# Weight sums and rotary products of the second layer moved from GpSimd to VectorE

## The chip, the cores and the metric

The kernel runs on one core of a Trainium2 chip. The core has five engines with instruction queues of their own, each executed in order: TensorE (matrix products, PE in the profile, its weight loads PEld), VectorE (DVE), ScalarE (ACT), GpSimd (POOL) and SyncE (SP, which issues the DMAs here). The metric is the device time of one execution in microseconds; the medians are over several runs.

## What is computed

One inference step of a two-layer encoder over 2048 prompt tokens and 32 sample tokens, model width 1024. Layer one is a gated delta rule; then one shared K and V are projected from the stream; layer two is sliding-window attention with its own query and gate projections. The part that matters here is the projection in front of layer two:

```python
kv = h @ w_kv                                   # 1024 -> 512 (K 256, V 256)
k = rope_partial(kv[..., :256].reshape(b, l, 4, 64), pos)
...
proj = x @ w_in                                 # 1024 -> 2048
q = rope_partial(proj[..., :1024].reshape(b, l, 16, 64), pos) * (64 ** -0.5)
z = proj[..., 1024:]                            # gate, used as silu(z)
...
rot = jnp.concatenate([x1 * cos - x2 * sin, x2 * cos + x1 * sin], -1)   # rope_partial, 16 of 64 dims
```

## The kernel before

Prompt and sample tokens are one matrix of 2080 rows, cut into five blocks of 416 columns once transposed. The projection multiplies 20 weight tiles (1024 x 128 each: two for K, two for V, eight for the queries, eight for the gate) with these blocks. Every fp32 product is made of three matmuls on rounded halves, high by high, high by low and low by high (`multiply`, L1685 to L1687); the high half is a rounding cast and the low half is the difference to it. For weights the cast is on ScalarE (`cast`, L1370, w_hi) and the difference on VectorE (`rest`, L1358, w_lo); for activations likewise (`operand`, L1443 and again L1358: tiles b11h, t4l and so on).

Four of the five blocks are done in two pairs by a seven-product scheme of the Strassen kind. Two weight tiles and a pair of blocks form one *group* (`group`): seven products P1 to P7 in place of eight, over sums of weights and sums of activations. The weight sums of a group are `sum6` (two additions into the tiles s1 and s2, both named s in the trace, L1492 and L1493), `sum7` (L1497, in place in w_raw) and `sum3` (L1501, in place in w_raw). The activation sums are made ahead (`presum`, L1401, GpSimd) and kept in memory as s_sums. There are 10 groups for each pair, 20 in all, and the fifth block is done by plain products in between (`single`).

The products accumulate in three PSUM banks, X, Y and Z. When one is ready, ScalarE copies it (`copied`, L1513) or VectorE adds it to an earlier copy (`added`, L1518), and `finish` sends the tile on: K and query tiles with rotated rows through `regroup` and `rope`, V tiles through a transpose (`turn`, L1747), gate tiles through a tanh and L1709. `rope` shuffles the rows (L1735, VectorE), multiplies the shuffled rows with the sine table (L1736, GpSimd) and the rows with the cosine table (L1737, VectorE), asks for the next table (L1727; its tile cs has one buffer) and adds both (L1741, VectorE).

The order is written out by hand: inside `manual_schedule` each engine executes its instructions in the order in which the program emits them. `stream` walks through the list of products. At product p it emits the weight fetch for products up to 12 ahead, the sums of product p + 5, the cast of p + 3 and the low half of p + 2, then the matmuls, then what follows a product (`after`), then two steps of side work (operands of the coming pair, activation sums), then what `delay` has made due. So a sum is emitted two products ahead of the cast that reads it, whichever engine makes it. Beside all this, 16 tiles of the output weights are split, with a difference on GpSimd (`out_weights`, L1675, shown under L1358 as wo_parts).

The first pair's operands are built while its first products run (about 1305 to 1350 us of the trace), the second pair's from about 1475 to 1518 us, and the last group ends near 1690 us; attention follows.

Of the kernel before, what the change touches and what calls it, by code (L numbers as in the profile page):

```python
# [15 lines left out]
ALU = mybir.AluOpType  # L16
# [1282 lines left out]
class P2:  # L1299
# [7 lines left out]
    K, V, Q, Z = 0, 2, 4, 12  # L1307
# [169 lines left out]
    def group(self, i, pair):  # L1477


        c, d = self.PAIRS[pair]  # L1480
        nc, V, P, f = self.nc, self.nc.vector, self.nc.gpsimd, self.scale(i)
        u = types.SimpleNamespace(tiles=(i, i + 1), raws=[], o={}, s={})
        a, b = slice(0, 4), slice(4, 8)

        def raw(n, ks):
            return lambda: u.raws[n][:, ks]

        def sum6():
            r1, r2 = u.raws
            for t in ("s1", "s2"):  # L1490
                u.s[t] = self.wsums.tile([128, 4, 128], F32, tag=t, name=t)
            P.tensor_tensor(out=u.s["s1"][:], in0=r2[:, a], in1=r2[:, b], op=ALU.add)  # L1492
            P.tensor_tensor(out=u.s["s2"][:], in0=u.s["s1"][:], in1=r1[:, a], op=ALU.subtract)  # L1493

        def sum7():
            r1, r2 = u.raws
            P.tensor_tensor(out=r2[:, a], in0=r1[:, a], in1=r2[:, a], op=ALU.subtract)  # L1497

        def sum3():
            r1, r2 = u.raws  # L1500
            P.tensor_tensor(out=r1[:, b], in0=r1[:, b], in1=u.s["s2"][:], op=ALU.subtract)  # L1501

        def bank(name):
            def get():
                if name not in u.o:
                    pool = {"X": self.px, "Y": self.py, "Z": self.pz}[name]
                    u.o[name] = pool.tile([128, 512], F32, tag=name, name=name)
                return u.o[name][:, :TB]
            return get

        def copied(key):
            t = u.o[key] = self.out()
            nc.scalar.activation(t[:], u.o["X"][:, :TB], AF.Copy, scale=f)  # L1513
            return t

        def added(name, key, j, b):
            t = u.o.pop(key)
            V.scalar_tensor_tensor(out=t[:], in0=u.o[name][:, :TB], scalar=f, in1=t[:], op0=ALU.mult, op1=ALU.add)  # L1518
            self.finish(t, j, b)

        def after7():
            copied("u3")
            self.delay(lambda: added("Z", "u3", i + 1, d), 1)

        def new(act, n, src, name, start, after=None, sum=None):
            return self.product(u, n, src, lambda: self.x[act], bank(name), start, True, after, sum, (pair, act))

        return {
            "P1": new("b11", (0,), raw(0, a), "X", True, lambda: copied("p1")),
            "P2": new("b21", (0,), raw(0, b), "Y", True, lambda: added("Y", "p1", i, c)),  # L1530
            "P6": new("t2", (0, 1), lambda: u.s["s2"][:], "X", False, lambda: copied("u2"), sum6),
            "P5": new("t1", (), lambda: u.s["s1"][:], "Z", True),
            "P7": new("t3", (0, 1), raw(1, a), "X", False, after7, sum7),
            "P4": new("t4", (1,), raw(1, b), "X", False, lambda: self.finish(copied("c"), i + 1, c)),
            "P3": new("b22", (0,), raw(0, b), "Z", False, lambda: added("Z", "u2", i, d), sum3)}

    def groups(self, pair):
# [191 lines left out]
    def rope(self, a, n):  # L1729
        nc, V, cs = self.nc, self.nc.vector, self.cs  # L1730
        s = self.out()
        mask = [(i + 8) % 16 + i // 16 * 16 for i in range(32)]

        def products():
            V.stream_shuffle(s[:n], a[:n], mask)  # L1735
            nc.gpsimd.tensor_tensor(out=s[:n], in0=s[:n], in1=cs[:n, 1, :], op=ALU.mult)  # L1736
            V.tensor_tensor(out=a[:n], in0=a[:n], in1=cs[:n, 0, :], op=ALU.mult)  # L1737
            self.load_tables()

        self.delay(products, 1)  # L1740
        self.delay(lambda: V.tensor_tensor(out=a[:n], in0=a[:n], in1=s[:n], op=ALU.add), 2)  # L1741
        return 3
# [839 lines left out]
```

## Time and profile before

| | us |
|---|---|
| median of 3 runs | 2078.54 |
| lowest and highest | 2074.08, 2079.13 |
| the profiled execution | 2077.04 |
| its span, first to last instruction | 2075.2 |
| granted TensorE clock, mean | 0.992 |

The profile gives each engine's busy time and share of the span. A row of the timeline has the start, the time taken, engine, line, operation, out<-in, the shape and, in brackets, how long the engine had been idle and which instruction released it; rows of like instructions that follow each other are merged, with the time from the first start to the last end. A row of the waits has the total, the number and the longest. A row of a tile has the minimum, median and maximum of one instruction in ns and the first and last start in us. PEclk is the clock that TensorE was granted, 1.00 being full speed.

### The profile page before, as it was taken

How to read it: one execution, taken by the hardware profiler on the slowest of the kernel's cores; microseconds unless marked ns; L12 is line 12 of the kernel's file. 1: busy time of each engine (PE TensorE's matmuls, PEld its weight loads, DVE VectorE, ACT ScalarE, POOL GpSimd, SP SyncE). 2: the span in 40 equal slices, each digit the busy share in tenths (PEclk: the TensorE clock that was granted, in tenths of full speed). 3: DMA queues.
4: the chain of work that ended last, by engine and by line, in shares of the span. 5: the costliest groups of instructions: out<-in, count | busy, mean ns of one | idle time of the engine just before them, and what ended most of it. 6: DMA issues, size and time to landing. Idle time of an engine off the chain costs nothing.

```text
span 2075.2 us, 36940 instructions
## 1 busy us (share of the span) xinstructions
PE 2023.8 (98%) x13518; PEld 1853.7 (89%) x13518; DVE 1483.4 (71%) x2580; ACT 994.0 (48%) x2445; POOL 907.5 (44%) x1248
## 2 busy tenths in 40 slices
PE   8999999999999999999899998899989999999998
PEld 6999999999999999999888887899989997777775
DVE  4686667675646778888887897887878755666565
ACT  4444443446532267777673222534634445555552
POOL 0222222222223167777760123387255524566665
PEclk9999999999999999999999999999999999999999
DMA  5122333237666545545864999788767679433321
GB/s 210 53 82 79 113 97 113 88 99 225 200 172 186 181 144 173 172 161 174 287 234 127 261 248 256 265 248 292 266 213 240 201 213 312 116 104 107 103 73 66
DMA packets 355541, 360.82 MB, mean 174 GB/s; under 512 B 157584, under 2 KB 280240, under 8 KB 355344
## 3 DMA queue, kind: packets, MB, share of 16 engines
q1 hardware_dynamic: 348880, 344.03, 54.1%
q10 hardware_dynamic: 6480, 14.44, 1.9%
q8 instruction: 106, 1.74, 0.3%
q14 instruction: 75, 0.61, 0.1%
HBM read 235.54 MB, written 134.06 MB: 178 GB/s over the span
## 4 chain that ended last, share of the span: by engine, by line
PE 75%; DVE 8%; DMA 7%; issue 3%; POOL 2%; SPq 2%; ACT 2%; DVEq 0%; POOLq 0%; ACTq 0%
PE ps L79 12%; PE ps L81 12%; PE ps L80 12%; PE ot L1136 3%; PE ot L1137 3%; PE ot L1138 3%; PE S L2029 2%; PE ot L2062 2%; PE tr L2044 2%; PE X L1687 2%; PE X L1685 2%; PE X L1686 2%; DMA r<-in_x 2%; PE g L698 2%; DMA act_raw<-s_sums 1%
## 5 line engine op out<-in xcount | busy, mean ns | idle before, releaser
L79 PE MATMUL ps<-act_hi,w_hi 128*128 128x416 f32 x1280 | 455.1, 356 | 0.0
L81 PE MATMUL ps<-act_hi,w_lo 128*128 128x416 f32 x1280 | 449.8, 352 | 0.0
L80 PE MATMUL ps<-act_lo,w_hi 128*128 128x416 f32 x1280 | 448.0, 350 | 0.0
L79 PEld LDWEIGHTS ps<-act_hi,w_hi 128*128 128x128 f32 x1280 | 240.3, 188 | 4.2 <-issue 0.6
L80 PEld LDWEIGHTS ps<-act_lo,w_hi 128*128 128x128 f32 x1280 | 240.7, 188 | 3.1
L81 PEld LDWEIGHTS ps<-act_hi,w_lo 128*128 128x128 f32 x1280 | 240.1, 188 | 3.3
L212 DVE SCALAR_TENSOR_TENSOR y<-R,convw,y 128x2083 f32<-128x2083 f32 x72 | 185.1, 2572 | 62.6 <-ACT y L209 46.7
L56 POOL TENSOR_TENSOR w_lo<-w_raw,w_hi 128x1024 fp32r<-128x1024 f32 x25 | 62.6, 2503 | 320.7 <-ACT w_hi L55 295.4
L732 POOL TENSOR_TENSOR tm<-L,Tt 128x60 f32<-128x60 f32 (+19 forms) x365 | 132.4, 363 | 83.9 <-issue 40.6
L1863 POOL TENSOR_TENSOR P<-e,sm 128x384 f32<-128x384 f32 (+2 forms) x128 | 102.5, 822 | 118.9 <-DVE sm L1853 112.7
L734 POOL TENSOR_TENSOR Tt<-Tt,tm 128x60 f32<-128x60 f32 (+19 forms) x365 | 141.3, 387 | 28.6
L1849 ACT ACTIVATE e<-S,nm 128x193 f32<-128x193 f32 (+2 forms) x260 | 104.8, 416 | 96.7 <-DVE nm L1844 58.1
L1358 DVE TENSOR_TENSOR w_lo<-w_raw,w_hi 128x512 fp32r<-128x512 f32 x132 | 141.6, 1089 | 8.8 <-POOL w_hi L1370 5.1
L308 ACT COPY R<-ps 128x416 f32<-128x416 f32 (+1 forms) x144 | 60.3, 442 | 105.7 <-PE ps L81 93.8
L1513 ACT ACTIVATE o<-X 128x416 f32<-128x416 f32 x80 | 41.5, 518 | 133.5 <-PE X L1687 133.4
L1136 PE MATMUL ot<-wo,g_hi 128*128 128x512 f32 x256 | 103.7, 405 | 0.0
L1137 PE MATMUL ot<-wo,g_hi 128*128 128x512 f32 x256 | 100.8, 394 | 0.0
L1138 PE MATMUL ot<-wo,g_lo 128*128 128x512 f32 x256 | 100.7, 394 | 0.0
L1370 ACT CAST w_hi<-w_raw 128x512 fp32r<-128x512 f32 x129 | 76.6, 615 | 17.3 <-POOL w_raw L1501 8.9
L218 DVE SCALAR_TENSOR_TENSOR y<-th,y 128x2083 f32<-128x2083 f32 x24 | 55.9, 2328 | 37.6 <-ACT th L216 37.6
L1844 DVE TENSOR_REDUCE nm<-S 128x4 f32<-128x772 f32 (+3 forms) x66 | 60.6, 918 | 15.3 <-PE S L2029 15.3
L216 ACT ACTIVATE th<-y 128x2083 f32<-128x2083 f32 x24 | 46.7, 1948 | 50.8 <-DVE y L212 47.6
(369 smaller groups left out, 5218.3 us busy)
## 6 DMA issues: line engine op xcount, KB each, us to landing
w_raw<-in_b_w SPq DMA_DIRECT2D x60, 512.0 KB
w_raw<-in_w_in SPq DMA_DIRECT2D x40, 512.0 KB
act_raw<-s_hT SPq DMA_DIRECT2D x64, 208.0 KB
s_rows<-o SPq DMA_DIRECT2D x50, 208.0 KB
k<-s_k SPq DMA_DIRECT2D x17, 512.0 KB
E<-s_E SPq DMA_DIRECT2D x17, 512.0 KB
s_hT<-hT SPq DMA_DIRECT2D x65, 128.0 KB
s_bq<-s_rows SPq DMA_DIRECT2D x40, 208.0 KB
```

Of the source, the lines that this page charges most:

```text
L79: nc.tensor.matmul(ps, hi[:, k, :], xh[:, k, :], start=(k == 0), stop=False)
L80: nc.tensor.matmul(ps, hi[:, k, :], xl[:, k, :], start=False, stop=False)
L81: nc.tensor.matmul(ps, lo[:, k, :], xh[:, k, :], start=False, stop=(k == KC - 1))
L212: nc.vector.scalar_tensor_tensor(out=y[:], in0=R[:, j:j + W], scalar=self.convw[:, i, j:j + 1], in1=y[:], op0=ALU.mult, op1=ALU.add)
L732: P.tensor_tensor(out=tm[:n, i0 - k:, :w], in0=L[:n, i0:, j:j + 1].to_broadcast(sh), in1=Tt[:n, j:j + 1, :w].to_broadcast(sh), op=ALU.mult)
L734: P.tensor_tensor(out=Tt[:n, i0:, :w], in0=Tt[:n, i0:, :w], in1=tm[:n, i0 - k:, :w], op=ALU.subtract)
L1136: nc.tensor.matmul(ps[:n], ghi[:, k, :n], hi, start=a, stop=False)
L1137: nc.tensor.matmul(ps[:n], ghi[:, k, :n], lo, start=False, stop=False)
L1138: nc.tensor.matmul(ps[:n], glo[:, k, :n], hi, start=False, stop=z)
L1358: P.tensor_tensor(out=lo, in0=raw, in1=hi, op=ALU.subtract)
L1849: self.nc.scalar.activation(x.e[:, h, u, :x.n], x.S[:, h, u, :], AF.Exp, bias=x.nm[:, h, u:u + 1], scale=1.0, accum_out=x.sm[:, h, u:u + 1])
L1863: self.nc.gpsimd.tensor_tensor(out=x.P[:, u, :nj * 128].rearrange("r (j h k) -> r j h k", h=2, k=64), in0=x.e[:, :, u, :n].rearrange("r h ...
```

## The change

The four weight sums of a group and the product with the sine table are issued on VectorE instead of GpSimd. Shapes, operands, buffers and the place in the program stay.

```diff
-        nc, V, P, f = self.nc, self.nc.vector, self.nc.gpsimd, self.scale(i)
+        nc, V, f = self.nc, self.nc.vector, self.scale(i)
...
-            P.tensor_tensor(out=u.s["s1"][:], in0=r2[:, a], in1=r2[:, b], op=ALU.add)
-            P.tensor_tensor(out=u.s["s2"][:], in0=u.s["s1"][:], in1=r1[:, a], op=ALU.subtract)
+            V.tensor_tensor(out=u.s["s1"][:], in0=r2[:, a], in1=r2[:, b], op=ALU.add)
+            V.tensor_tensor(out=u.s["s2"][:], in0=u.s["s1"][:], in1=r1[:, a], op=ALU.subtract)
...
-            P.tensor_tensor(out=r2[:, a], in0=r1[:, a], in1=r2[:, a], op=ALU.subtract)
+            V.tensor_tensor(out=r2[:, a], in0=r1[:, a], in1=r2[:, a], op=ALU.subtract)
...
-            P.tensor_tensor(out=r1[:, b], in0=r1[:, b], in1=u.s["s2"][:], op=ALU.subtract)
+            V.tensor_tensor(out=r1[:, b], in0=r1[:, b], in1=u.s["s2"][:], op=ALU.subtract)
...
             V.stream_shuffle(s[:n], a[:n], mask)
-            nc.gpsimd.tensor_tensor(out=s[:n], in0=s[:n], in1=cs[:n, 1, :], op=ALU.mult)
+            V.tensor_tensor(out=s[:n], in0=s[:n], in1=cs[:n, 1, :], op=ALU.mult)
             V.tensor_tensor(out=a[:n], in0=a[:n], in1=cs[:n, 0, :], op=ALU.mult)
```

VectorE's queue in the first pair, where the last operands (t4l) are made and the second group's first sums fall due (about 1335 us of the trace before; s_14079 and s_14080 are that group's s1 and s2):

```order
 L1735 STREAM_SHUFFLE o<-o 64x416
+L1736 TENSOR_TENSOR o<-o,cs 64x416
 L1737 TENSOR_TENSOR o<-o,cs 64x416
 L1358 TENSOR_TENSOR w_lo<-w_raw,w_hi 128x512
 L1358 TENSOR_TENSOR t4l<-act_raw,t4h 128x416 x2
 L1741 TENSOR_TENSOR o<-o 64x416
+L1492 TENSOR_TENSOR s_14079<-w_raw 128x512
+L1493 TENSOR_TENSOR s_14080<-s_14079,w_raw 128x512
 L1358 TENSOR_TENSOR w_lo<-w_raw,w_hi 128x512
```

The product stands between the shuffle and L1737, and the two sums stand ahead of the next low half.

VectorE's queue of the changed kernel at the end of the second pair's operands (about 1507 us of the trace before), ahead of which stands the last L1709:

```order
L1735 STREAM_SHUFFLE o<-o 64x416
L1736 TENSOR_TENSOR o<-o,cs 64x416
L1737 TENSOR_TENSOR o<-o,cs 64x416
L1358 TENSOR_TENSOR w_lo<-w_raw,w_hi 128x512
L1358 TENSOR_TENSOR t4l<-act_raw,t4h 128x416 x2
L1741 TENSOR_TENSOR o<-o 64x416
L1358 TENSOR_TENSOR w_lo<-w_raw,w_hi 128x512
L1358 TENSOR_TENSOR t4l<-act_raw,t4h 128x416
```

Against before, only L1736 is new in these rows; the next two sums come behind the four b22l that follow.

GpSimd's queue in the first pair (about 1414 to 1430 us), with the s1 and s2 of one group as s_14931 and s_14932:

```order
 L1401 TENSOR_TENSOR act_raw<-act_raw 128x416 x2
 L1358 TENSOR_TENSOR wo_parts<-wo_parts 128x512
-L1736 TENSOR_TENSOR o<-o,cs 128x416
-L1501 TENSOR_TENSOR w_raw<-w_raw,s_14768 128x512
-L1492 TENSOR_TENSOR s_14931<-w_raw 128x512
-L1493 TENSOR_TENSOR s_14932<-s_14931,w_raw 128x512
-L1497 TENSOR_TENSOR w_raw<-w_raw 128x512
 L1401 TENSOR_TENSOR act_raw<-act_raw 128x416 x2
 L1358 TENSOR_TENSOR wo_parts<-wo_parts 128x512
```

Activation sums and output weights follow each other directly, and nothing else is left in that stretch. The queues of TensorE, ScalarE and SyncE are the same before and after.

## The prediction

> **What bounds the kernel now.** I read the page first, then the busy time by stretch, then what TensorE waits for, then both engines of the change in order of time.
>
> ```profile
> span 2075.2 us, 36940 instructions
> PE 2023.8 (98%) x13518; PEld 1853.7 (89%) x13518; DVE 1483.4 (71%) x2580; ACT 994.0 (48%) x2445; POOL 907.5 (44%) x1248
> ```
>
> TensorE sets the time. The change can only win what TensorE loses in the stage that holds the edited lines. Busy time by stretch (PE, PEld, DVE, ACT, POOL, granted clock, DMA share, GB/s):
>
> ```profile
> 1335.00:1352.00 17.00, 12.41 (x56) 11.38 (x55) 13.84 (x18) 7.78 (x16) 7.49 (x4) 0.90 0.90 316
> 1415.00:1447.00 32.00, 30.93 (x158) 28.93 (x157) 24.86 (x24) 14.03 (x28) 22.75 (x16) 1.00 0.84 293
> 1475.00:1505.00 30.00, 29.38 (x154) 28.17 (x153) 23.82 (x42) 21.29 (x45) 3.77 (x3) 1.00 0.85 281
> 1505.00:1520.00 15.00, 9.56 (x41) 8.62 (x40) 13.74 (x21) 7.54 (x15) 4.84 (x3) 0.89 0.72 225
> 1535.00:1543.00 8.00, 5.79 (x29) 5.06 (x29) 5.09 (x7) 2.18 (x4) 5.95 (x3) 1.00 0.36 111
> 1543.00:1690.00 147.00, 147.00 (x780) 145.62 (x779) 109.64 (x132) 64.06 (x126) 75.62 (x50) 1.00 0.67 210
> ```
>
> The last row gives TensorE's undisturbed pace: 147.00 / 780 = 0.1885 us a matmul. A stretch loses its length less its matmuls times 0.1885: 17 - 56 x 0.1885 = 6.4; 2.2; 1.0; 7.3; 2.5. Together **19.4 us, the ceiling**. From 1543 on nothing is lost, so there a later GpSimd or VectorE costs and wins nothing. Who holds TensorE up between 1300 and 1700:
>
> ```profile
> PE X L1687 <- DVE w_lo L1358: 5.5, 4, 2.5
> PE ps L1687 <- DVE w_lo L1358: 5.4, 2, 2.8
> PE Z L1685 <- DVE o L1518: 2.7, 2, 2.1
> ```
>
> VectorE, late with the low halves of the weights and with emptying bank Z. Why it is late shows in the instructions on the weights (minimum/median/maximum ns), in GpSimd's product, and in a VectorE line that reads one operand from PSUM:
>
> ```profile
> L1358 DVE TENSOR_TENSOR w_lo<-w_raw,w_hi x132: 640/686/1808, 1304.6 to 1727.3; 128x512 fp32r<-128x512 f32 x132
> L1492 POOL TENSOR_TENSOR s<-w_raw x20: 1279/1642/1754, 1315.5 to 1658.8; 128x512 f32<-128x512 f32 x20
> L1501 POOL TENSOR_TENSOR w_raw<-w_raw,s x20: 1289/1677/1753, 1325.8 to 1670.2; 128x512 f32<-128x512 f32 x20
> L1736 POOL TENSOR_TENSOR o<-o,cs x15: 1485/1503/2097, 1335.4 to 1612.9; 128x416 f32<-128x416 f32 x10, 64x416 f32<-64x416 f32 x5
> L1518 DVE SCALAR_TENSOR_TENSOR o<-Z,o x40: 575/591/593, 1345.4 to 1688.8; 128x416 f32<-128x416 f32 x40
> ```
>
> The same subtraction takes 0.64 or 1.81 us, while L1518 never stretches: a VectorE operation with two SBUF inputs stands still while GpSimd runs one. The place at 1335, on VectorE, GpSimd, ScalarE and TensorE:
>
> ```profile
> 1334.60 0.62 DVE L1735 STREAM_SHUFFLE o<-o 64x416 f32<-64x416 f32 x1
> 1335.26 0.58 DVE L1737 TENSOR_TENSOR o<-o,cs 64x416 f32<-64x416 f32 x1
> 1335.77 0.68 DVE L1358 TENSOR_TENSOR w_lo<-w_raw,w_hi 128x512 fp32r<-128x512 f32 x1
> 1336.37 4.30 DVE L1358 TENSOR_TENSOR t4l<-act_raw,t4h 128x416 fp32r<-128x416 f32 x2
> 1340.60 0.57 DVE L1741 TENSOR_TENSOR o<-o 64x416 f32<-64x416 f32 x1
> 1341.10 0.67 DVE L1358 TENSOR_TENSOR w_lo<-w_raw,w_hi 128x512 fp32r<-128x512 f32 x1
> 1345.40 0.58 DVE L1518 SCALAR_TENSOR_TENSOR o<-Z,o 128x416 f32<-128x416 f32 x1
> ```
> ```profile
> 1335.36 2.04 POOL L1736 TENSOR_TENSOR o<-o,cs 64x416 f32<-64x416 f32 x1 [8.23 <-DMA act_raw<-s_hT]
> 1338.73 1.50 POOL L1493 TENSOR_TENSOR s<-s,w_raw 128x512 f32<-128x512 f32 x1
> ```
> ```profile
> 1341.19 0.61 ACT L1370 CAST w_hi<-w_raw 128x512 fp32r<-128x512 f32 x1
> ```
> ```profile
> 1341.82 0.46 PE L1687 MATMUL X<-t4h,w_lo 128*128 128x416 f32 x1 [2.53 <-DVE w_lo L1358]
> 1346.13 0.43 PE L1685 MATMUL Z<-b22h,w_hi 128*128 128x416 f32 x1 [2.06 <-DVE o L1518]
> ```
>
> Two t4l subtractions need 4.30 us (1.0 without company) because GpSimd operations run one after another through them (the first and the third are shown).
>
> **The change, part by part.** Twenty groups have four sums each, and there are 15 products: 95 instructions leave GpSimd. None issues a DMA; the order of ScalarE, SP and TensorE stays.
>
> *Price on VectorE.* No sum on VectorE is in this trace; the same shape, two SBUF inputs, is w_lo, whose successor starts 0.60 us after it (1335.77, 1336.37). A 416-wide operation costs 0.50 to 0.51 (1340.60, 1341.10). Where the second reads what the first wrote, it waits for the end, as L1741 would: 0.69 for the sum pair. So 80 x 0.62 + 15 x 0.51 = 57 us more on VectorE. From below, the stillness goes: 80 x 1.6 + 15 x 1.5 = 150 us of GpSimd, which now can hold up VectorE, vanish. Net cost on VectorE's clock: from +57 (nothing was overlapped) to -93 (all of it was). The nearest rows are the place above, where 4.30 against 1.0 shows most of it overlapped; so I take VectorE as freer on the whole, and price the path place by place.
>
> The Trainium skill speaks against 0.60: "VectorE: DVE Perf Modes", "The DRAIN you can't avoid", lets the next operation start only when the pipe is empty. That would make the step 0.69 and add some 7 us of VectorE work over all sums; the rows above show starts 0.60 apart, so the trace does not agree for independent operations.
>
> *Place 1335.* Now: shuffle 1334.60, L1736 1335.26, L1737 1335.77, w_lo 1336.28, two t4l from 1336.88, L1741 1337.89, the two sums 1338.39 and 1339.08, w_lo 1339.68. That is 1.4 us before 1341.10, though two sums stand in front: the stall of 2.53 shrinks to 1.1. Then a t4l, a b22l, and w_lo, whose cast ends at 1341.80; two b22l; L1518 at 1343.4 instead of 1345.40. Bank Z is free **2.0 us earlier**. TensorE also ran at half rate after these stalls:
>
> ```profile
> 1347.40:1351.10 3.70, 3.70 (x13) 3.57 (x12) 1.47 (x3) 0.00 (x0) 0.00 (x0) 0.54 0.97 321
> 1515.00:1518.20 3.20, 3.20 (x11) 3.03 (x11) 3.20 (x7) 1.73 (x4) 0.00 (x0) 0.50 0.82 222
> ```
>
> 3.70 - 13 x 0.1885 = 1.2 us and 3.20 - 11 x 0.1885 = 1.1 us. With stalls of 1.1 and 1.7 in place of 2.5 and 2.1 I take the slow stretch here as gone: together 2.8 us, and the stretch at 1535 loses 2.5 us at a clock of 1.00. Gain 3.2; at least 2.0, at most 6.4.
>
> *Place 1415.* VectorE:
>
> ```profile
> 1419.42 1.58 DVE L1358 TENSOR_TENSOR w_lo<-w_raw,w_hi 128x512 fp32r<-128x512 f32 x1
> 1420.92 1.68 DVE L1741 TENSOR_TENSOR o<-o 128x416 f32<-128x416 f32 x1
> 1422.52 3.46 DVE L1358 TENSOR_TENSOR w_lo<-w_raw,w_hi 128x512 fp32r<-128x512 f32 x2
> ```
>
> Three locked operations of about 1.6 become 0.6, 0.5 and 0.6, and a product (0.5) and a sum (0.6) come in front: some 2 us earlier, so the stall on w_lo goes. Other bits of the 2.2 wait for the 16 casts and loads of the output weights, untouched. Gain 1.6 (0 to 2.2). *Place 1475*: GpSimd is busy 3.77 of 30 us, nothing to unlock: 0 (a sum in front of a w_lo could cost 0.6).
>
> *Place 1505*, VectorE and TensorE:
>
> ```profile
> 1508.40 0.68 DVE L1358 TENSOR_TENSOR w_lo<-w_raw,w_hi 128x512 fp32r<-128x512 f32 x1
> 1509.00 4.30 DVE L1358 TENSOR_TENSOR t4l<-act_raw,t4h 128x416 fp32r<-128x416 f32 x2
> 1513.72 0.68 DVE L1358 TENSOR_TENSOR w_lo<-w_raw,w_hi 128x512 fp32r<-128x512 f32 x1
> ```
> ```profile
> 1514.45 0.46 PE L1687 MATMUL ps<-act_hi,w_lo 128*128 128x416 f32 x1 [2.78 <-DVE w_lo L1358]
> ```
>
> The w_lo at 1508.40 comes 0.5 **later** (L1736 now stands ahead, and everything behind waits). The next: two t4l 1509.5, L1741 1510.5, w_lo 1511.0 instead of 1513.72, and no sums stand there (they moved behind b22l). Its stall of 2.8 goes, and the 1.1 of slow clock with it: 2.8 + 1.1 - 0.5 = gain 3.4 (1.5 to 6.5).
>
> *Place 1535*, VectorE:
>
> ```profile
> 1536.94 0.58 DVE L1737 TENSOR_TENSOR o<-o,cs 64x416 f32<-64x416 f32 x1 [5.11 <-DMA cs<-in_cs]
> 1539.10 1.66 DVE L1741 TENSOR_TENSOR o<-o 64x416 f32<-64x416 f32 x1 [0.97 <-POOL o L1736]
> 1540.69 1.28 DVE L1358 TENSOR_TENSOR w_lo<-w_raw,w_hi 128x512 fp32r<-128x512 f32 x2
> ```
>
> VectorE waits for the table's load before and after; L1736 adds 0.5 ahead of w_lo, but the table's only buffer comes free about as much earlier. Then L1741 at 1538.0, two sums, w_lo at 1539.8 instead of 1540.69: gain 0.8 (-0.5 to 2.5).
>
> *Sum*: 3.2 + 1.6 + 0 + 3.4 + 0.8 = **9.0 us**. The profiled execution took 2077.04 us (span plus 1.84), 1.5 below the median 2078.54; the same gain from the median gives **2069.5 us**. Cover that could go: on VectorE a sum that waits for its weights' load holds up the w_lo, t4l or L1518 behind it, and TensorE behind those. Loads are asked for up to 12 products ahead, 12 x 12 x 0.1885 = 27 us, so I price that at nothing; a load that late would cost its whole wait.
>
> **The rivals.**
>
> *The order on VectorE decides (slower).* If w_lo stretches for another reason than GpSimd's sums, 57 us are added to an engine that is busy 109.64 of the 147 us even in its calm stretch, and each of 20 sum pairs stands 0.69 + 0.60 = 1.3 us in front of a w_lo. If half of that is not to spare, 20 x 0.65 = 13 us, 2091.5. It decides if the mean of w_lo stays over 1 us. Against it: L1518's 575 to 593. Chance 0.06.
>
> *Loads decide (no change).* The five places have DMA shares up to 0.90 and the 5.11 us wait for the table. If VectorE merely waits for loads where it waited for GpSimd, 1.6 + 0.8 stay: 2076. Against: the rows between 1336 and 1341 wait for GpSimd, not for a landing. Chance 0.18.
>
> *The half rate stays.* The first stall at 1505 grows to 3.5 us, and a slow stretch may now follow it alone: 1.1 less, 2070.6. The Trainium skill ("TensorE: Matmul & The Clock Gate", "The HAM clock gate") puts the drop after an idle window of about 3.4 us; the trace agrees only partly: it dropped after 2.53 and 2.06 us in a row. Chance 0.16.
>
> *All stalls go*: later loads are asked for earlier too; 17 of the 19.4: 2061.5. Chance 0.15.
>
> **How the numbers follow.** The forecast has 0.45. About 0.3%, 6.2 us, is what a measurement of this kernel can tell from no change. Faster than 2072.3: forecast, half rate and all stalls, less their tails: 0.74. Same: 0.20. Slower: 0.06. The range leaves out the slower rival and the far tails: low 2061 (all stalls), high 2077 (loads decide, and a little noise).
>
> **What would show it.** w_lo's maximum falls near 0.7 save beside the 32 GpSimd operations that stay (sums of activations, output weights); VectorE's t4l pairs take 1 us; the waits for w_lo halve; the stall before bank Z at the first t4 product is under 2 us; that at the second pass's first single is about 0.5 longer. Wrong: w_lo's mean still 1.1, TensorE waiting for new sums (s on VectorE), or new stalls after 1543.

## The result and the profile after

The changed kernel took 2071.66 us (median of 14 runs, 2067.87 to 2076.28), the kernel before beside it 2077.9 us (14 runs, 2071.08 to 2082.43). The ratio is 0.9974, with an interval of 0.9965 to 0.9984: faster by 5.4 us by the ratio, 6.2 by the medians. The sign is certain. The size is about what I had called the least that can be told from no change, and short of the 9.0 forecast. The profiled execution took 2075.11 us, with a span of 2073.3.

The page's engine line of the changed kernel:

```profile
span 2073.3 us, 36854 instructions
PE 2025.7 (98%) x13518; PEld 1856.9 (90%) x13518; DVE 1467.3 (71%) x2675; ACT 991.7 (48%) x2445; POOL 755.2 (36%) x1153
```

VectorE has 95 more instructions than before (2675 against 2580) and yet is busy 16.1 us less (1467.3 against 1483.4). The minimum, median and maximum in ns of the operations on the weights show why:

```profile
L1358 DVE TENSOR_TENSOR w_lo<-w_raw,w_hi x132: 647/684/1792, 1307.5 to 1724.2; 128x512 fp32r<-128x512 f32 x132
L1492 DVE TENSOR_TENSOR s<-w_raw x20: 640/684/1767, 1323.4 to 1660.3; 128x512 f32<-128x512 f32 x20
L1493 DVE TENSOR_TENSOR s<-s,w_raw x20: 691/692/1662, 1324.1 to 1661.0; 128x512 f32<-128x512 f32 x20
```

A sum that took GpSimd 1.6 us takes VectorE 0.68. The maxima near 1.8 us remain, beside the GpSimd operations that stay: of the 172 low halves w_lo between 1300 and 1730 us, 74 took over 0.9 us before and 18 do after, and each of these overlaps a GpSimd operation. What this does to the means shows in the groups by form between 1315 and 1690 us (count, busy us, mean ns, idle time before them), first of the kernel before:

```profile
L1358 DVE TENSOR_TENSOR w_lo<-w_raw,w_hi 128x512 fp32r<-128x512 f32 x117 | 129.1, 1120 | 3.7 <-ACT w_hi L1370 3.7
L1358 DVE TENSOR_TENSOR t4l<-act_raw,t4h 128x416 fp32r<-128x416 f32 x8 | 12.0, 1521 | 2.3 <-ACT t4h L1443 2.3
```

and of the changed kernel:

```profile
L1358 DVE TENSOR_TENSOR w_lo<-w_raw,w_hi 128x512 fp32r<-128x512 f32 x121 | 87.6, 740 | 1.9 <-ACT w_hi L1370 1.9
L1358 DVE TENSOR_TENSOR t4l<-act_raw,t4h 128x416 fp32r<-128x416 f32 x8 | 4.5, 582 | 1.5 <-ACT t4h L1443 1.5
```

The mean of w_lo fell from 1120 to 740 ns, that of t4l from 1521 to 582. Now the stretches of the prediction, moved with the work, since the same instruction comes at another time (same columns as there):

```profile
1337.00:1352.00 15.00, 13.41 (x71) 12.63 (x70) 13.27 (x25) 8.00 (x17) 0.48 (x1) 1.00 0.92 328
1411.00:1443.00 32.00, 32.00 (x170) 31.45 (x169) 23.61 (x36) 13.10 (x26) 8.01 (x6) 1.00 0.84 293
1471.00:1501.00 30.00, 29.06 (x151) 27.68 (x151) 23.78 (x44) 21.27 (x45) 1.30 (x1) 1.00 0.86 275
1501.00:1515.00 14.00, 11.16 (x52) 10.62 (x52) 11.48 (x23) 8.28 (x17) 0.00 (x0) 0.88 0.89 279
1528.00:1540.00 12.00, 8.76 (x32) 8.11 (x31) 8.07 (x12) 2.68 (x5) 1.78 (x1) 0.72 0.46 150
1540.00:1687.00 147.00, 147.00 (x780) 145.76 (x779) 100.98 (x169) 63.10 (x125) 10.83 (x9) 1.00 0.65 207
```

Each stretch less its matmuls times 0.1885 us gives what TensorE lost there:

| place | lost before | lost after | won | forecast |
|---|---|---|---|---|
| 1335 | 6.4 | 1.6 | 4.8 | 3.2 |
| 1415 | 2.2 | 0.0 | 2.2 | 1.6 |
| 1475 | 1.0 | 1.5 | -0.5 | 0 |
| 1505 | 7.3 | 4.2 | 3.1 | 3.4 |
| 1535 | 2.5 | 6.0 | **-3.5** | 0.8 |
| sum | 19.4 | 13.3 | 6.1 | 9.0 |

The sum, 6.1 us, is close to the difference of the medians, 6.2. The two profiled executions as a whole differ by only 1.9 us (2077.04 and 2075.11): the changed kernel's came into this stage 3.2 us behind and lost 0.9 us more after it, where nothing was edited. Four places come out within 1.6 us of their terms, and the fifth has the wrong sign. The calm stretch (last row) still loses nothing, now with POOL busy 10.83 us where it was 75.62. TensorE's waits between 1300 and 1700 us:

```profile
PE X L1687 <- DVE w_lo L1358: 3.5, 2, 3.2
PE ps L1687 <- DVE w_lo L1358: 3.2, 2, 2.8
PE Z L1685 <- DVE o L1518: 1.9, 2, 1.3
```

Nearly all that is left of the waits for w_lo is two long ones, 3.2 and 2.8 us. In the first pair (place 1335), VectorE in order of time:

```profile
1336.90 0.62 DVE L1735 STREAM_SHUFFLE o<-o 64x416 f32<-64x416 f32 x1
1337.56 0.58 DVE L1736 TENSOR_TENSOR o<-o,cs 64x416 f32<-64x416 f32 x1
1338.07 0.58 DVE L1737 TENSOR_TENSOR o<-o,cs 64x416 f32<-64x416 f32 x1
1338.57 0.68 DVE L1358 TENSOR_TENSOR w_lo<-w_raw,w_hi 128x512 fp32r<-128x512 f32 x1
1339.17 1.08 DVE L1358 TENSOR_TENSOR t4l<-act_raw,t4h 128x416 fp32r<-128x416 f32 x2
1340.17 0.58 DVE L1741 TENSOR_TENSOR o<-o 64x416 f32<-64x416 f32 x1
1340.68 0.68 DVE L1492 TENSOR_TENSOR s<-w_raw 128x512 f32<-128x512 f32 x1
1341.39 0.69 DVE L1493 TENSOR_TENSOR s<-s,w_raw 128x512 f32<-128x512 f32 x1
1342.00 0.68 DVE L1358 TENSOR_TENSOR w_lo<-w_raw,w_hi 128x512 fp32r<-128x512 f32 x1
```

From the shuffle to the last w_lo 5.10 us, worked out beforehand as 5.08; it was 6.50 before, without the product and the two sums. The t4l pair takes 1.08 us, not 4.30. At place 1505, the first stall on TensorE in the kernel before and the same one after, with the two matmuls behind it:

```profile
1509.13 0.46 PE L1687 MATMUL ps<-act_hi,w_lo 128*128 128x416 f32 x1 [2.66 <-DVE w_lo L1358]
```
```profile
1506.18 0.71 PE L1687 MATMUL ps<-act_hi,w_lo 128*128 128x416 f32 x1 [2.84 <-DVE w_lo L1358]
1506.69 0.55 PE L1685 MATMUL ps<-act_hi,w_hi 128*128 128x416 f32 x1
1507.04 0.55 PE L1686 MATMUL ps<-act_lo,w_hi 128*128 128x416 f32 x1
```

The second stall of before (2.78 us) is gone, the first stays, and matmuls 0.35 us apart follow it, where an undisturbed one takes 0.1885: the half rate. Now the place that failed, which comes at about 1530. VectorE of the changed kernel:

```profile
1525.54 0.62 DVE L1735 STREAM_SHUFFLE o<-o 64x416 f32<-64x416 f32 x1
1531.90 0.58 DVE L1736 TENSOR_TENSOR o<-o,cs 64x416 f32<-64x416 f32 x1 [5.74 <-DMA cs<-in_cs]
1532.41 0.58 DVE L1737 TENSOR_TENSOR o<-o,cs 64x416 f32<-64x416 f32 x1
1532.91 0.68 DVE L1358 TENSOR_TENSOR w_lo<-w_raw,w_hi 128x512 fp32r<-128x512 f32 x1
```

TensorE, and the issue of the table on SyncE's queue, of the changed kernel:

```profile
1530.05 0.35 PE L1686 MATMUL X<-b11l,w_hi 128*128 128x416 f32 x1
1533.64 0.71 PE L1687 MATMUL X<-b11h,w_lo 128*128 128x416 f32 x1 [3.24 <-DVE w_lo L1358]
```
```profile
1523.41 0.55 SPq L1727 DMA_DIRECT2D cs<-in_cs  x1
```

and the same instructions of the kernel before:

```profile
1536.33 0.35 PE L1686 MATMUL X<-b11l,w_hi 128*128 128x416 f32 x1
1538.18 0.45 PE L1687 MATMUL X<-b11h,w_lo 128*128 128x416 f32 x1 [1.50 <-DVE w_lo L1358]
```
```profile
1528.49 0.59 SPq L1727 DMA_DIRECT2D cs<-in_cs  x1
```

TensorE arrives 6.28 us earlier (1536.33 to 1530.05). The table is asked for 5.08 earlier and takes as long to its first use (8.49 us against 8.45, the first use before being L1737 at 1536.94), so it is there only 5.04 earlier. The gap in TensorE grows from 1.85 to 3.59 us, by 1.74: 1.24 from the table, 0.51 from the product that now stands ahead of w_lo. Half rate follows, which the shorter gap did not bring: 19 matmuls in the 6.40 us from 1533.60 on, 2.8 us too long.

### The profile page after: what moved, and what is told of

The parts are those of the page before. It is cut to its first block, busy times and chain, and to the rows that moved or that the text cites. A ratio compares the mean times of both kernels' runs of the same rounds, so it can differ in the third digit from the quotient of the medians.

```text
span 2073.3 us, 36854 instructions
## 1 busy us (share of the span) xinstructions
PE 2025.7 (98%) x13518; PEld 1856.9 (90%) x13518; DVE 1467.3 (71%) x2675; ACT 991.7 (48%) x2445; POOL 755.2 (36%) x1153
## 3 DMA queue, kind: packets, MB, share of 16 engines
q8 instruction: 106, 1.74, 0.3%
## 4 chain that ended last, share of the span: by engine, by line
PE 80%; DMA 7%; DVE 7%; SPq 2%; ACT 2%; issue 1%; POOL 0%; DVEq 0%; POOLq 0%
PE ps L79 12%; PE ps L81 12%; PE ps L80 12%; PE ot L1136 3%; PE ot L1137 3%; PE ot L1138 3%; PE X L1687 3%; PE X L1685 3%; PE X L1686 3%; PE S L2029 2%; PE tr L2044 2%; PE ot L2062 2%; PE g L698 2%; DMA r<-in_x 1%; PE ks L849 1%
## 5 line engine op out<-in xcount | busy, mean ns | idle before, releaser
L1358 POOL TENSOR_TENSOR wo_parts<-wo_parts 128x512 fp32r<-128x512 f32 x16 | 22.0, 1376 | 243.9 <-ACT wo_parts L1674 233.1
L1358 DVE TENSOR_TENSOR w_lo<-w_raw,w_hi 128x512 fp32r<-128x512 f32 x132 | 97.4, 752 | 6.7 <-POOL w_hi L1370 4.7
L1401 POOL TENSOR_TENSOR act_raw<-act_raw 128x416 f32<-128x416 f32 x32 | 43.5, 1359 | 111.4 <-DMA act_raw<-s_hT 108.5
```

Of the source, the lines that this page charges most:

```text
L1358: P.tensor_tensor(out=lo, in0=raw, in1=hi, op=ALU.subtract)
```

## The experiments

Three accounts were open. The theory (A): VectorE's operations with two SBUF inputs stand still while GpSimd works; the change ends that, and the next bound is the table's load. The rivals: the 95 operations more on VectorE are what decides, whatever GpSimd does (B); or the loads of operands, weights and tables together set the pace, so that a stall taken away in one place comes back in another (C). The recorded expectations use the letters less strictly: "Theory B" of the first one is account C here, and "Rival B" of pool_busy is a fourth account, that sums and products are ready sooner. The kernels of a group ran on one chip and share its runs of the kernel before; ratios, with their intervals, are against that.

| group, run | median us (runs) | before us (runs) | ratio | interval |
|---|---|---|---|---|
| 1 changed kernel again | 2070.39 (9) | 2076.06 (13) | 0.9979 | 0.9969 to 0.9989 |
| 1 pool_busy | 2089.42 (5) | | 1.0069 | 1.0056 to 1.0082 |
| 1 vector_busy | 2126.71 (4) | | 1.0242 | 1.0228 to 1.0256 |
| 1 left_out | 2065.80 (5) | | 0.9949 | 0.9936 to 0.9963 |
| 2 two_tables | 2066.62 (5) | 2075.91 (23) | 0.9948 | 0.9936 to 0.9961 |
| 2 one_table_wk10 | 2068.41 (5) | | 0.9960 | 0.9946 to 0.9973 |
| 2 sums_only | 2074.14 (11) | | 0.9990 | 0.9981 to 0.9999 |
| 2 products_only | 2074.59 (12) | | 0.9989 | 0.9980 to 0.9998 |
| 3 lead3 | 2072.94 (11) | 2076.22 (32) | 0.9988 | 0.9978 to 0.9997 |
| 3 lead3_two | 2067.11 (9) | | 0.9959 | 0.9945 to 0.9974 |
| 3 lead3_before | 2077.12 (11) | | 1.0005 | 0.9994 to 1.0016 |
| 3 before_wk10 | 2076.12 (11) | | 1.0001 | 0.9992 to 1.0011 |

**The changed kernel again**, for a second profile.

> The changed kernel again, as the yardstick for the others on this chip. Theory A (GpSimd's sums held VectorE up; 8 to 10 us were won up to 1525 us and some 3.5 given back at the rotary table's load near 1530) expects 5 to 7 us below the kernel before, with a TensorE stall of 3 to 4 us at the first w_lo after the table's load. Theory B (loads decide, the lock matters little) expects 0 to 4 us below and no such stall in a fixed place.

2070.39 us, 5.7 below before, as A expected. The pattern repeats: aligned by the same copy to SBUF (L1470), it is 8.65 us ahead of before at 1525 us and 4.45 ahead at the end of the stage; what was won in front is partly given back at the table (a gap of 4.77 us there). It came into the stage 1.6 us behind, so the stage is worth 6.1 us here, and 6.0 in the first profile. The stall at the second pair's t4 is there too, with one difference:

```profile
1501.66 0.35 PE L1686 MATMUL ps<-act_lo,w_hi 128*128 128x416 f32 x1
1504.87 0.46 PE L1687 MATMUL ps<-act_hi,w_lo 128*128 128x416 f32 x1 [2.85 <-DVE w_lo L1358]
1505.16 0.35 PE L1685 MATMUL ps<-act_hi,w_hi 128*128 128x416 f32 x1
```

A stall of 2.85 us, and the matmul after the next comes 0.19 us later, not 0.35: no half rate here.

**GpSimd kept busy for nobody.** The changed kernel, with as many GpSimd operations as it lost, on a tile that nothing else uses.

```diff
+    def beside_sum(self, n):
+        d = self.idle[:, :n]
+        self.nc.gpsimd.tensor_tensor(out=d, in0=d, in1=d, op=ALU.subtract)
...
             V.tensor_tensor(out=u.s["s2"][:], in0=u.s["s1"][:], in1=r1[:, a], op=ALU.subtract)
+            self.beside_sum(512)
+            self.beside_sum(512)
```

The other two sums and the product get one such operation each.

> The changed kernel, and beside each sum and product on VectorE an operation of the same size on GpSimd over a tile of zeros that nothing else uses. Nobody waits for it, so no hand-over comes back, only GpSimd's use of its memory port. Theory A: w_lo stretches again (mean over 1.0 us instead of about 0.75), VectorE has 57 us more work than before the change and the old standstill on top, so TensorE waits for it again: 5 to 40 us slower than the kernel before. Rival B (the gain came from sums and products that are ready sooner, 0.7 instead of 1.6 us and without a hand-over between engines): as the changed kernel, 5 to 7 us faster than before.

2089.42 us, 13.4 above before, as A expected, and 19.0 above the changed kernel on the same chip. The groups of this kernel, 1315 to 1700 us (L1360 is L1358 of the others, L1499 is L1493):

```profile
L1360 DVE TENSOR_TENSOR w_lo<-w_raw,w_hi 128x512 fp32r<-128x512 f32 x116 | 103.4, 906 | 2.0 <-ACT w_hi L1372 2.0
L1481 POOL TENSOR_TENSOR idle<-idle 128x512 f32<-128x512 f32 x76 | 103.9, 1367 | 4.4
L1499 DVE TENSOR_TENSOR s<-s,w_raw 128x512 f32<-128x512 f32 x20 | 19.5, 973 | 0.7
```

and its waits on TensorE:

```profile
PE X L1697 <- DVE w_lo L1360: 14.4, 11, 4.1
PE ps L1697 <- DVE w_lo L1360: 4.0, 5, 1.6
```

No tile of this work depends on the idle one, yet w_lo stretches from 740 to 906 ns (over 1.0 us was expected) and TensorE waits for it 16 times instead of 4. The sums and products are on VectorE here as in the changed kernel, without a hand-over between engines, so that alone is not what won. What costs is that the two engines work at once, not who waits for GpSimd's results. The Trainium skill says as much ("SBUF — State Buffer", "Terms": VectorE and GpSimd share one pair of ports, held for a whole instruction). The trace agrees as to operations with two SBUF inputs, and t4l at 582 against 1521 ns is the price of it here.

**VectorE kept busy for nobody.** The kernel before, with the same idle operations on VectorE beside GpSimd's real sums and products; the cut shows the helper against that of pool_busy.

```diff
-        self.nc.gpsimd.tensor_tensor(out=d, in0=d, in1=d, op=ALU.subtract)
+        self.nc.vector.tensor_tensor(out=d, in0=d, in1=d, op=ALU.subtract)
```

> The kernel before, and beside each sum and product on GpSimd an operation of the same size on VectorE over a tile of zeros. It prices the 57 us that the change puts on VectorE without the relief. Theory A: each of these also stands still beside GpSimd, so it costs up to 1.7 us: 5 to 40 us slower than before. If VectorE had room to spare in this stage (rival: the load on VectorE is free): within 2 us of before.

2126.71 us, 50.6 above before, beyond what was expected. A group of it and the wait of TensorE that is largest in total:

```profile
L1481 DVE TENSOR_TENSOR idle<-idle 128x512 f32<-128x512 f32 x73 | 79.4, 1088 | 0.6
```
```profile
PE X L1697 <- DVE w_lo L1360: 41.3, 25, 4.9
```

The added operations stretch too (1088 ns), and TensorE waits for w_lo 25 times. So VectorE has nothing to spare while GpSimd works beside it, and account B's price is real: 13.4 us in pool_busy, about the 13 that the prediction gave it, and far more here. Most of it isn't paid in the changed kernel, where GpSimd's sums are gone from beside VectorE. Why this costs 37 us more than pool_busy, with as many operations on each engine, is open; one difference is that here the real sums and products, on which casts and rotations wait, are GpSimd's.

**The work left out.**

```diff
-            "P6": new("t2", (0, 1), lambda: u.s["s2"][:], "X", False, lambda: copied("u2"), sum6)
+            "P6": new("t2", (0, 1), raw(0, a), "X", False, lambda: copied("u2"))
...
-            nc.gpsimd.tensor_tensor(out=s[:n], in0=s[:n], in1=cs[:n, 1, :], op=ALU.mult)
```

P5 takes raw(1, a) likewise, and sum7 and sum3 go.

> The kernel before with the weight sums and the sine products left out altogether (the products use plain weight halves instead of sums, so the second layer is not computed), which gives the relief without the 57 us. Theory A: the stalls at 1335, 1415 and 1510 go as with the change or more, the wait for the rotary table stays, since ropes still ask for tables: 6 to 10 us faster than before, 0 to 4 better than the changed kernel. If the work on VectorE is what limits the changed kernel: 12 us or more faster than before.

2065.80 us: 10.3 below before, 4.6 below the changed kernel, a little outside what was expected. So the most that taking these operations off GpSimd can give is about 10 us, and VectorE's doing them, with the casts' waits for the sums, takes back 4 to 5 of it. The wait for the table stays in the waits of this kernel on VectorE, with nothing left of sums or sine products (its L1736 is the cosine product):

```profile
DVE o L1736 <- DMA cs<-in_cs: 6.9, 2, 5.7
```

But TensorE gives nothing back there: it is 9.6 us ahead of before at 1525 us and 10.1 at the end of the stage. The table's issue came 9.0 us earlier than before (1519.50), so TensorE's gap is 2.45 us, and no half rate follows. The changed kernel's loss at the table is thus not the price of the load alone, but of an issue that came less early than TensorE.

**Two tables.** The changed kernel with two buffers for cs, each asked for one rotation earlier; for their space, output tiles go from 11 to 10. Two controls have the 10 tiles alone, in the changed kernel (one_table_wk10) and in the kernel before (before_wk10).

```diff
-            self.cs = self.tab.tile([128, 2, TB], F32, tag="cs", name="cs")
+            self.tabs.append(self.tab.tile([128, 2, TB], F32, tag="cs", name="cs", bufs=2))
...
-        self.wk = new_pool(tc, right, "p2_wk", 11, side="right")
+        self.wk = new_pool(tc, right, "p2_wk", 10, side="right")
```

> The changed kernel with two buffers for the rotary table, each table asked for one rope earlier; to make room the ring of output tiles has 10 instead of 11 buffers. Theory A, second half (the table's load near 1530 gives back 3 to 5 us of the gain): the stall before the first w_lo there, 3.4 to 4.6 us with a slow clock behind it, goes; 3 to 6 us faster than the changed kernel, 9 to 12 us below the kernel before. Rival C (the load only stands in for the general rate of the loads, which set the pace): another load is late there, within 1.5 us of the changed kernel.

> The control of the run with two tables: the changed kernel with 10 instead of 11 output tiles and one table. If the missing tile costs nothing: as the changed kernel, 5 to 6 us below the kernel before. If it costs: slower than that by what two tables would have to be credited with.

> The kernel before with 10 instead of 11 output tiles, the control for the runs with 10 tiles. If a tile less is without effect: within 1.5 us of the kernel before, and the 1.9 us by which the changed kernel with 10 tiles came out faster than with 11 is within what these measurements scatter. If it helps (fewer stores in flight): 2 to 4 us below.

2066.62 us with two tables, 2068.41 for the control: the second table is worth 1.8 us where I expected 3 to 6 against the changed kernel, and the intervals overlap. The control is 7.5 us below before, where 5 to 6 were expected. Ten tiles change nothing in the kernel before (1.0001), so the 2 us more aren't shown to be theirs. Two stretches of the kernel with two tables:

```profile
1500.00:1514.00 14.00, 10.85 (x44) 10.04 (x43) 11.28 (x22) 7.73 (x16) 0.00 (x0) 0.76 0.84 265
1522.00:1537.00 15.00, 15.00 (x81) 14.88 (x80) 11.84 (x20) 6.69 (x14) 1.29 (x1) 1.00 0.89 265
```

Around 1530 nothing is lost any more (81 x 0.1885 = 15.3), so the table was what TensorE waited for there. From 1525 us to the end of the stage this profile gains 2.8 us on the kernel before, where the control's gives back 2.2, 5.0 apart. But the stretch in front of it, at the second pair's operands, now loses 14 - 44 x 0.1885 = 5.7 us against 4.2 in the changed kernel. That isn't shown to be C: TensorE's gap there is 3.50 us against 3.19, the rest is slow clock (0.76 against 0.88), and the changed kernel's second profile, at full clock, loses 14 - 59 x 0.1885 = 2.9 in the same stretch. Why the medians show only 1.8 us of these 5.0 is open. This is the fastest by median of the kernels that do the whole work, 9.3 us below before.

**Each half alone.** The changed kernel with the product back on GpSimd (sums_only), and the kernel before with only the product on VectorE (products_only).

```diff
-            V.tensor_tensor(out=s[:n], in0=s[:n], in1=cs[:n, 1, :], op=ALU.mult)
+            nc.gpsimd.tensor_tensor(out=s[:n], in0=s[:n], in1=cs[:n, 1, :], op=ALU.mult)
```

> Only the weight sums on VectorE, the sine product stays on GpSimd. Theory A: the place near 1510 keeps part of its stall, since the product of 2.1 us still holds up the pair of t4l subtractions there, the rest is as in the changed kernel: 3 to 6 us below the kernel before. If the product's hand-over is what mattered: within 2 us of before.

> Only the sine product on VectorE, the sums stay on GpSimd. Theory A: 130 of 155 us of GpSimd work stay and hold VectorE up, with 8 us more work there: within 2 us of the kernel before. If the product's hand-over is what mattered: 4 to 6 us below.

1.8 us below before for the sums, a miss (3 to 6 were expected), and 1.3 for the products, as expected. Together 3.1, against 4.4 to 5.4 by the two ratios of the whole change. One wait of each says where it went. TensorE in the kernel with the sums alone:

```profile
1532.44 0.72 PE L1687 MATMUL X<-b11h,w_lo 128*128 128x416 f32 x1 [4.12 <-DVE w_lo L1358]
```

TensorE in the kernel with the products alone:

```profile
1505.91 0.72 PE L1687 MATMUL ps<-act_hi,w_lo 128*128 128x416 f32 x1 [4.99 <-DVE w_lo L1358]
```

With the sums alone the stall at the table is the longest, as in the whole change, and one of 2.51 us is left at the second pair's operands. With the products alone there is one of 4.99 us at these operands, where the kernel before has 2.66 and 2.78. So the sums are what relieves the operands, and the gain is given back at the table. That the halves add up to less than the whole isn't shown: the intervals (about 2 us each way) allow a plain sum.

**More lead.** Sums, casts and low halves each one product earlier (6, 4 and 3 products ahead), in the changed kernel, in that with two tables and in the kernel before.

```diff
-    FETCH, SUM, CAST, SUB, STEPS = 12, 5, 3, 2, 2
+    FETCH, SUM, CAST, SUB, STEPS = 12, 6, 4, 3, 2
```

> The changed kernel with every weight sum, cast and low half emitted one product (2.26 us) earlier: 6, 4 and 3 products ahead instead of 5, 3 and 2. What stays of the stalls after the change, near 1505 and 1530, are low halves that stand in VectorE's queue behind an operation that waits for a load. Theory A expects those stalls to shrink by up to 2.3 us each with the slow clock behind the second: 3 to 7 us below the changed kernel, 9 to 12 below the kernel before. Rival C (the loads' rate sets the pace): the stalls move to the operands themselves, within 1.5 us of the changed kernel.

> The same with two buffers for the rotary table and 10 output tiles. Theory A: both late places relieved, 10 to 14 us below the kernel before. Rival C: no better than two tables alone, 8 to 10 us below.

> The kernel before (sums and products on GpSimd) with sums, casts and low halves one product earlier. If an earlier low half alone repairs the stalls, the engine of the sums mattered little: 5 to 10 us below the kernel before. Theory A: VectorE still stands still beside GpSimd, but its low halves have 2.26 us more to spare, so part of the same stalls goes: 2 to 6 us below, and lead3 is at least 4 us faster than this.

If VectorE's lateness were all, an earlier low half should win. It doesn't: 0.9988 against 0.9974 and 0.9979 for the changed kernel, 0.9959 against 0.9948 for two tables, 1.0005 for before. Two stretches of the changed kernel with more lead:

```profile
1508.00:1518.00 10.00, 5.68 (x24) 5.19 (x23) 5.80 (x12) 3.67 (x7) 0.00 (x0) 0.85 0.46 134
1530.00:1542.00 12.00, 7.53 (x29) 7.00 (x29) 7.95 (x12) 3.52 (x7) 1.26 (x1) 0.73 0.44 145
```

10 - 24 x 0.1885 = 5.5 and 12 - 29 x 0.1885 = 6.5 us are lost in the two places alone, with VectorE busy 5.80 of 10 and 7.95 of 12 us: it isn't out of time there, it waits. In the first place the w_lo stands behind a b22l whose cast on ScalarE waited 5.07 us for the load of its block; in the second VectorE waits 5.64 us for the table. A's expectations fail for all three kernels. C's fits better: lead3_two is 9.1 us below before (8 to 10), with a gap of 4.45 us left at the operands, but lead3 came out 2 to 3 us slower than the changed kernel by the ratios, where C allowed 1.5, and the intervals overlap. That lead3_before wins nothing had not been expected either way. What remains of A is the difference between the two kernels with the same lead: 2077.12 less 2072.94, 4.2 us for the change (at least 4 were expected).

## Why the prediction was right, and where not

*The stillness of VectorE* was read rightly: pool_busy brings it back with work that nobody waits for, t4l pairs take 1.08 us where 1 was forecast, and the mean of w_lo is far under the 1.1 us that would have refuted it. TensorE's waits for w_lo fell from 10.9 to 6.7 us, less than by the half that I named, since the table's stall grew. VectorE's net cost, bounded between +57 and -93 us, came out at -16.1 us of busy time in the whole kernel.

*The steps on VectorE* held to a tenth: 0.51 for the product, 0.60 to 0.61 for a sum, 0.71 for the first sum of a pair, and 5.10 us for the whole piece at 1335 where I had 5.08. The rule that the prediction set against 0.60, that an operation starts only when the pipe is empty, is as little borne out by the new sums as by the rows of before. The same section of the Trainium skill ("VectorE: DVE Perf Modes", "The DRAIN you can't avoid") says that a next operation which isn't held starts earlier, which the prediction left out and these rows fit.

*Place 1335* won 4.8 us for 3.2: the slow clock went entirely (1.00), the first stall of 2.53 us all but went (1.1 was forecast), and the stall before bank Z fell to 1.3 us (under 2 was forecast). *Place 1415* won all of its 2.2 (1.6). *Place 1475* lost 0.5, within the 0.6 that I had named.

*Place 1505* won 3.1 for 3.4. The second stall went as worked out; the first grew from 2.66 to 2.84 us, by 0.2 where 0.5 was feared. The slow clock, of which 1.1 us were counted as won, did not go in this profile, as the half-rate rival had it; in the second profile of the same kernel it did. So that the total comes within 0.3 is in part luck.

*Place 1535* is the step that failed: "the table's only buffer comes free about as much earlier". It comes free 5.1 us earlier, and TensorE stands there 6.3 us earlier. In the twelve profiles with one table, this one takes 7.7 (vector_busy) to 8.7 us from its issue to its first use, however early it is asked for. I had worked out every place from its own rows of before, as if each kept its own clock. But all that is won at 1335, 1415 and 1505 arrives together at the next load, and the load moves only by what its issue moves: by 5.1 us here, and by 9.0 in left_out, which gives nothing back there. The term was +0.8 and measured -3.5: 1.24 for the table, 0.51 for the product in front of w_lo (which I had) and the half rate, 2.8, that follows a gap of 3.59 us and had not followed one of 1.85; less some 0.8 us of smaller losses behind the gap of before (2.5 less 1.7). two_tables, with nothing lost there, shows the table as the cause in that place.

*The rivals.* "Loads decide" was priced too low and had the wrong reason: it let 1.6 + 0.8 us of gain stay, at two places, and 6.2 were measured; 9.5 us were won by 1525 us in the first profile (3.2 us behind there at the stage's start, 6.3 ahead at 1525) and 3.5 given back after it. It was right in that a load, the table's, takes back part of the gain. "All stalls go" is out: 13.3 of the 19.4 us stay. "The order on VectorE decides" is what happens where the stillness doesn't end: pool_busy is 13.4 us slower than before, vector_busy 50.6. *VectorE's added work*, which the prediction counted only as steps ahead of single low halves, costs 4 to 5 us by left_out. *New waits for sums* and stalls after 1543 did not appear.

*Not settled*: what sets the 8.5 us that the table takes from its issue to its use, and with it the pace of the loads at the second pair's operands; the table ahead of it takes 3.5 us from issue to use in both profiles (1523.25 to 1526.73, 1518.18 to 1521.69). C is shown by more lead as stalls that move, not as a mechanism.

## What to carry to other kernels

Moving work from GpSimd to VectorE can leave VectorE with less to do, where it stood still beside that work: the test is a line whose minimum and maximum differ by 2 to 3 times (0.64 and 1.81 us here), while a line with a PSUM operand doesn't vary (575 to 593 ns). A gain that is added up stall by stall must be carried along: what is won in front arrives at the next load, and a load with one buffer comes earlier only by as much as its issue does. Price the last places of a chain with the sum of the gains ahead of them.

## What the hardware showed beside this

The length of a stall doesn't tell whether the half rate follows. In the profile of the changed kernel it followed a stall of 2.84 us (the next matmuls 0.35 us apart), in the second profile it didn't follow one of 2.85 at the same place (0.19 apart). The Trainium skill ("TensorE: Matmul & The Clock Gate", "The HAM clock gate") has the clock watched in a window that runs freely, of some 3.4 us. That fits two outcomes of like stalls, but no run here shows the window.

An engine's idle work isn't free here: 95 operations that nobody waits for cost 19.0 us on GpSimd beside the changed kernel, and 50.6 us on VectorE beside the kernel before.
